# Down projections whose partial sums collect in PSUM, copied out by ScalarE, with weights fetched six steps ahead

## The chip, the cores and the metric

The kernel runs on one core of one Trainium2 chip. The metric is device time in microseconds (us). The kernel before takes 1835.76 us, the median of three runs (1833.45 to 1837.6).

The core has a matrix engine (PE; weight loads are listed as PEld), a vector engine (DVE), a scalar engine (ACT), GpSimd (POOL) and SyncE (SP), which here issues all DMA. Matrix products land in PSUM, which has 8 banks of 128x512 f32. The program names them by what they mostly hold: three `mm`, one `o`, two `y`, two `tp`.

## The reference

One layer of a decoder trunk on a 1024x1024 activation: a gated feed-forward block (FFN), a token mixer with two kinds of attention, a second FFN, each followed by a residual sum and a layer norm (LN). The part that is changed is the last product of each FFN and the sum and LN behind it:

```
def swiglu(h, w_gate, w_up, w_down):
    return (jax.nn.silu(h @ w_gate) * (h @ w_up)) @ w_down
...
        h = modulate(x, sh1, sc1)
        y = swiglu(h, ffn1_w_gate[l], ffn1_w_up[l], ffn1_w_down[l])
        x = layer_norm(ALPHA * x + (1 + g1) * (MACARON * y), ln1_g[l], ln1_b[l])
        h = modulate(x, sh2, sc2)
        y = token_mix(h, w_in[l], b_forget[l], swa_sinks[l], grp_gain[l], w_out[l])
        x = layer_norm(ALPHA * x + (1 + g2) * y, ln2_g[l], ln2_b[l])
        h = modulate(x, sh3, sc3)
        y = swiglu(h, ffn2_w_gate[l], ffn2_w_up[l], ffn2_w_down[l])
        x = layer_norm(ALPHA * x + (1 + g3) * (MACARON * y), ln3_g[l], ln3_b[l])
```

`w_down` has 2816 rows and 1024 columns.

## The kernel before

All large products run as three matmuls of rounded pieces (`mm3`, L105): each operand is split by `split` (L101) into a rounded high part (ACT cast, L102) and a remainder (DVE subtraction, L103), and high x high, high x low and low x high are added in PSUM.

`down` is called once for each FFN (at about 448 us and 1603 us of the trace). It computes A @ B with A = 1024x2816 (stored transposed in device memory, `aT`) and B = `w_down`, as a 2x2 block product in seven half-size products in place of eight. The blocks of A are A11 to A22, of B B11 to B22; S1 to S4 and T1 to T4 are sums of them. This document numbers the products P1 = A11·B11, P2 = A12·B21, P3 = S4·B22, P4 = A22·T4, P5 = S1·T1, P6 = S2·T2, P7 = S3·T3. The results are C11 = P1+P2 (left columns, first 512 tokens), C12 = P1+P6+P5+P3 (right columns, first 512 tokens), C21 = P1+P6+P7 with P4 added or subtracted by the sign of T4 (left columns, last 512 tokens) and C22 = P1+P6+P7+P5 (right columns, last 512 tokens).

Each product has 11 steps (`NG`, one for each 128 rows of the inner dimension), and a step is 4 output banks x 3 matmuls of 128x512. In the last product the last `tail` steps (2 in the first call, 7 in the second) are run bank by bank, so that bank 0 is complete first. A step's operands are made by `operands`: a DMA of an `aT` tile into ring `u`, a DMA or a sum for the weight tile, and two splits into rings `z` (4 buffers) and `w` (6). `get` records the operands one step ahead (`LOOK`), three from the sixth product on. T2, T1 and T4 are made in place over the weight tiles by `weight`.

In the kernel before the order is P1, P2, P3, P6, P5, P7, P4, and the bank sets alternate between products (`PBANKS`). Every product is evicted by itself at its end, bank by bank: P1 and P3 with an ACT copy (L477), the others with one or two DVE sums of PSUM and a 128x2048 SBUF tile (`x1`, `x2`, `x3`, `u4`). Finished results are put on a list `todo`, from which one entry is popped after each step: `add_to` (L420) multiplies by the gate (L423) and adds to the residual (L424); then come the LN of the first 512 tokens (`steps1` in the first call, `final_a` in the second). After the loop the caller does the LN of the last 512 tokens: in the first call `ln_steps` between the blocks of the V projection (L741 to L778), in the second `final_b` (L1302), with which the program ends. `ln_stats` takes two `bn_stats` (left and right half), `bn_aggr`, an epsilon, and a power on POOL.

The order of instructions on each engine is set before the run by the layer that builds the program, from the order in which they are recorded, the buffers' releases and its own estimates; every engine, SP too, then runs its list strictly in that order.

Of the kernel before, what the change touches and what calls it, by code (L numbers as in the profile page):

```python
# [14 lines left out]
P = 128  # L15
# [31 lines left out]
def layer_kernel(ctx, tc, xT, x, c, adaT, adab, wg1, wu1, wd1, wqk, wv1, wv2, bf, sinks,  # L47
# [57 lines left out]
    def mm3(o, lh, ll, rh, rl, start, stop):  # L105
        T.matmul(o, lh, rh, start=start, stop=False)  # L106
        T.matmul(o, lh, rl, start=False, stop=False)  # L107
        T.matmul(o, ll, rh, start=False, stop=stop)  # L108
# [46 lines left out]
    def ln_stats(src):  # L155

        s6 = small([P, 2, 6], "bn", 4)
        V.bn_stats(s6[:, 0], src[:, :HT])
        V.bn_stats(s6[:, 1], src[:, HT:])
        mv = small([P, 2], "mv", 4)  # L160
        V.bn_aggr(mv, s6)
        ve = small([P, 1], "ve", 4)
# [5 lines left out]
    def ln_norm(src):  # L168
        mv, rs = ln_stats(src)
        V.tensor_scalar(src, src, mv[:, 0:1], rs, op0=ALU.subtract, op1=ALU.mult)  # L170
# [194 lines left out]
    def down(ai, wd, gate, alpha, load, steps_a, tail=TAIL):  # L365
# [4 lines left out]
        sums = {}  # L370
# [15 lines left out]

        def weight(kind, g):
            if kind in ("B11", "B21", "B22"):
                return home(kind, g)
            if kind == "T2":  # L390
                b12 = home("B12", g)
                b11, b21, b22 = (raw[k, 0, g] for k in ("B11", "B21", "B22"))
# [10 lines left out]
            return raw[{"T1": "B11", "T3": "B12", "T4": "B21"}[kind], 0, g]  # L403
# [13 lines left out]
        def stash():  # L417
            return st("h", [P, 4, HT])

        def add_to(xt, k, n, s, eng=V):  # L420

            y = xt[k][:, cols[n]]
            eng.tensor_tensor(s, s, gate[:, cols[n]], ALU.mult)  # L423
            V.scalar_tensor_tensor(y, y, alpha, s, op0=ALU.mult, op1=ALU.add)  # L424
# [16 lines left out]
        xs = []  # L441
        for i in range(7):
            banks = [psum(q) for q in PBANKS[2 if i == 6 and not ai else i % 2].split()]

            def mul(a, w, g, k):
                mm3(banks[k], a[:, 0, k * P:(k + 1) * P], a[:, 1, k * P:(k + 1) * P], w[:, 0], w[:, 1],
                    g == 0, g == NG - 1)

            tl = tail if i == 6 else 1
            for g in range(NG - tl):  # L450
                a, w = get(i, g)
                for k in range(4):
                    mul(a, w, g, k)
                if i in (0, 4) and 2 <= g < 6:
                    if g == 2:
                        xs.append([])
                    xs[-1].append(load(i // 4, g - 2))
                if todo:
                    for f in todo.pop(0):
                        f()  # L460
            aw = [get(i, g) for g in range(NG - tl, NG)]
            if i in (0, 1, 2, 4):
                new = stash()
                if i == 0:
                    x1 = new
                elif i == 1:
                    x2 = new
                elif i == 2:
                    x3 = new
                else:  # L470
                    u4 = new
            for k in range(4):
                for j in range(tl):
                    mul(*aw[j], NG - tl + j, k)
                b = banks[k]
                if i in (0, 2):
                    A.copy(new[:, k], b)  # L477
                elif i in (1, 4):
                    V.tensor_tensor(new[:, k], x1[:, k], b, ALU.add)
                    if i == 4:  # L480
                        V.tensor_tensor(x3[:, k], x3[:, k], b, ALU.add)
                elif i == 3:
                    V.tensor_tensor(x1[:, k], x1[:, k], b, ALU.add)
                elif i == 5:
                    V.tensor_tensor(u4[:, k], u4[:, k], b, ALU.add)
                    V.tensor_tensor(x1[:, k], x1[:, k], b, ALU.add)
                else:
                    s = xs[1][k][:, cols[0]]
                    if not ai:
                        V.tensor_tensor(b, b, gate[:, cols[0]], ALU.mult)  # L490
                    V.tensor_tensor(s, s, b, ALU.subtract)
            if i == 1:
                todo = [[lambda k=k: add_to(xs[0], k, 0, x2[:, k])] for k in range(4)]
            elif i == 3:
                todo = [[lambda k=k: V.tensor_tensor(x3[:, k], x3[:, k], x1[:, k], ALU.add)] for k in range(4)]
            elif i == 4:
                todo = [[lambda k=k: add_to(xs[0], k, 1, x3[:, k])] for k in range(4)] + steps_a(xs[0])
            elif i == 5:
                z = [[lambda k=k, n=n: add_to(xs[1], k, n, (x1, u4)[n][:, k], V)] for n in range(2) for k in range(4)]
                for j in range(8):  # L500
                    if j < len(todo):
                        todo[j] = z[j] + todo[j]
                    else:
                        todo.append(z[j])
        while todo:
            for f in todo.pop(0):
                f()
# [172 lines left out]
    def ln_steps(zt, hf, m, dst, split_to, park=None):  # L680

        def norm(k):
            ln_norm(zt[k])
# [37 lines left out]
    def steps1(z):  # L721
# [5 lines left out]
              steps1)  # L727
# [548 lines left out]
    def final_a(zt):  # L1276
# [3 lines left out]
        def stats(k):  # L1280
# [3 lines left out]
            s1, s2, nm, ve = (q[:, j:j + 1] for q in [small([P, 2, 6], "bn", 4)[:, 0]] for j in range(4))  # L1284
# [18 lines left out]
    def final_b(zt):  # L1303
# [20 lines left out]
        for k in range(4):  # L1324
            sc[k] = ln_stats(zt[k])
# [3 lines left out]
    final_b(down(1, wd2, gate_load(2), 1.0, load_x2, final_a, 7))  # L1329
# [59 lines left out]
```

## Time and profile before

| | |
|---|---|
| median of 3 runs | 1835.76 us |
| the profiled execution's own time | 1834.09 us |
| its span, first to last instruction | 1832.1 us |
| granted PE clock, mean over the span | 0.985 of full |
| busy: PE / DVE / ACT | 1755.3 / 1546.1 / 764.7 us |

Busy time is the time in which at least one instruction of the engine is under way. Matmuls overlap: in a dense stretch they start 0.227 us apart and each is shown as 0.39 us long, so a busy PE has no visible gap, and gaps show as a duration in brackets with what ended them. DVE operations on 128x512 start 0.60 us apart and are shown as 0.69 us long.

### The profile page before, as it was taken

The page shows a single profiled execution, that of the slowest core. Times are in us where ns is not written, and L with a number is a line of the kernel's source. Part 1 is how long each engine was busy: PE and PEld are TensorE (multiplying, and loading weights), DVE is VectorE, ACT ScalarE, POOL GpSimd, SP SyncE. Part 2 cuts the span into 40 slices and gives each one's busy share as a digit, 9 for nine tenths or more (in the row PEclk, how much of TensorE's full clock was granted, in tenths as well). Part 3 has the DMA queues.
Part 4 walks back from the last instruction along what each step waited for, and adds up shares of the span by engine and source line. Part 5 has one row for each costly group of instructions (what it writes and reads, how often), then busy time and mean ns, then how long its engine had stood idle before and what let it go on. Part 6 is the DMA issues. An engine that isn't in the chain of part 4 may idle for free.

```text
span 1832.1 us, 23557 instructions
## 1 busy us (share of the span) xinstructions
PE 1755.3 (96%) x8114; PEld 1444.7 (79%) x8114; DVE 1546.1 (84%) x2805; ACT 764.7 (42%) x1465; POOL 23.0 (1%) x32
## 2 busy tenths in 40 slices
PE   7999999999999989999889899999999999999995
PEld 5788888888888879877667777778888888888884
DVE  7999999999597995378678797899788887878999
ACT  5432333233544442277356461543233333344480
POOL 0000000000000000000000000000000000000000
PEclk9999999999999999999989999999999999999998
DMA  9355555558754245855958863333223232675442
GB/s 360 127 197 178 193 193 193 170 173 290 233 167 143 86 134 180 242 148 154 229 143 198 215 205 107 138 109 128 97 99 131 88 108 92 223 231 166 133 144 80
DMA packets 163175, 303.44 MB, mean 166 GB/s; under 512 B 15384, under 2 KB 47728, under 8 KB 163056
## 3 DMA queue, kind: packets, MB, share of 16 engines
q1 hardware_dynamic: 163056, 301.94, 52.1%
q8 instruction: 64, 1.05, 0.2%
q14 instruction: 55, 0.45, 0.1%
HBM read 224.17 MB, written 77.71 MB: 165 GB/s over the span
## 4 chain that ended last, share of the span: by engine, by line
PE 73%; DVE 15%; DMA 6%; ACT 3%; issue 2%; SPq 0%; POOL 0%; DVEq 0%; ACTq 0%; POOLq 0%
PE y L106 10%; PE y L107 10%; PE y L108 10%; PE mm L106 9%; PE mm L108 9%; PE mm L107 9%; PE o L106 3%; PE o L108 3%; PE o L107 3%; DVE w L103 2%; DVE h L103 2%; DMA q<-cum_d 2%; PE tp L107 1%; PE tp L108 1%; PE tp L1114 1%
## 5 line engine op out<-in xcount | busy, mean ns | idle before, releaser
L102 ACT CAST w<-u 128x512 fp32r<-128x512 f32 x303 | 186.6, 622 | 393.1 <-PE y L108 160.2
L106 PE MATMUL y<-h,w 128*128 128x512 f32 x728 | 287.7, 395 | 5.0 <-ACT h L102 2.1
L107 PE MATMUL y<-h,w 128*128 128x512 f32 x728 | 285.6, 392 | 0.0
L108 PE MATMUL y<-h,w 128*128 128x512 f32 x728 | 285.2, 392 | 0.0
L103 DVE TENSOR_TENSOR w<-u,w 128x512 fp32r<-128x512 f32 x303 | 206.5, 686 | 23.4 <-ACT w L102 22.1
L106 PE MATMUL mm<-h,w 128*128 128x512 f32 x528 | 207.7, 394 | 18.7 <-ACT h L102 15.6
L107 PE MATMUL mm<-h,w 128*128 128x512 f32 x528 | 206.7, 392 | 0.3 <-DVE h L103 0.2
L108 PE MATMUL mm<-h,w 128*128 128x512 f32 x528 | 206.7, 392 | 0.0
L106 PEld LDWEIGHTS y<-h,w 128*128 128x128 f32 x728 | 137.5, 189 | 33.5 <-ACT h L102 2.5
L108 PEld LDWEIGHTS y<-h,w 128*128 128x128 f32 x728 | 137.0, 188 | 26.6
L107 PEld LDWEIGHTS y<-h,w 128*128 128x128 f32 x728 | 137.0, 188 | 26.3
L102 ACT CAST w<-t 128x512 fp32r<-128x512 f32 x106 | 65.5, 621 | 185.1 <-PE mm L108 70.3
L106 PEld LDWEIGHTS mm<-h,w 128*128 128x128 f32 x528 | 100.2, 190 | 40.9 <-ACT h L102 16.0
L107 PEld LDWEIGHTS mm<-h,w 128*128 128x128 f32 x528 | 100.0, 189 | 22.2 <-DVE h L103 1.5
L108 PEld LDWEIGHTS mm<-h,w 128*128 128x128 f32 x528 | 99.9, 189 | 21.3 <-DVE w L103 1.0
L102 ACT CAST z<-u 128x512 fp32r<-128x512 f32 x88 | 54.8, 623 | 105.2 <-PE y L108 46.8
L103 DVE TENSOR_TENSOR z<-u,z 128x512 fp32r<-128x512 f32 x88 | 60.5, 689 | 35.7 <-ACT z L102 35.6
L103 DVE TENSOR_TENSOR t<-tp,t 128x512 fp32r<-128x512 f32 (+1 forms) x126 | 72.8, 586 | 18.4 <-ACT t L102 17.7
L102 ACT CAST t<-tp 128x512 fp32r<-128x512 f32 (+1 forms) x126 | 61.8, 502 | 48.3 <-PE tp L1114 47.4
L102 ACT CAST w<-h 128x512 fp32r<-128x512 f32 x111 | 68.2, 617 | 29.4 <-PE o L108 10.5
L103 DVE TENSOR_TENSOR w<-h,w 128x512 fp32r<-128x512 f32 x111 | 75.6, 686 | 1.8 <-ACT w L102 1.8
L103 DVE TENSOR_TENSOR w<-t,w 128x512 fp32r<-128x512 f32 x106 | 72.8, 689 | 1.4 <-ACT w L102 0.8
(356 smaller groups left out, 3948.1 us busy)
## 6 DMA issues: line engine op xcount, KB each, us to landing
u<-aT SPq DMA_DIRECT2D x154, 256.0 KB, 2.7
q<-in_adaT SPq DMA_DIRECT2D x56, 512.0 KB, 3.4
u<-in_wg SPq DMA_DIRECT2D x92, 256.0 KB, 3.0
u<-in_wu SPq DMA_DIRECT2D x90, 256.0 KB, 2.8
aT<-z SPq DMA_DIRECT2D x44, 512.0 KB, 3.2
h<-in_wd SPq DMA_DIRECT2D x88, 256.0 KB, 4.5
qkd<-w SPq DMA_DIRECT2D x26, 512.0 KB, 4.1
aT<-b SPq DMA_DIRECT2D x22, 512.0 KB, 4.2
```

The lines of the kernel that those rows point to most:

```text
L102: A.copy(hi, src)
L103: V.tensor_tensor(lo, src, hi.bitcast(F32), ALU.subtract)
L106: T.matmul(o, lh, rh, start=start, stop=False)
L107: T.matmul(o, lh, rl, start=False, stop=False)
L108: T.matmul(o, ll, rh, start=False, stop=stop)
L1114: T.transpose(pt[:, tok(i - q0)], sps[i][:, tok(j)], ident)
```

## The change

The products run in the order P1, P2, P6, P5, P3, P7, P4. Bank set 0 (`tp tp y y`) takes P1; then P6, P5 and P3 are added into the same four banks without a restart, so that they hold P1, P1+P6, P1+P6+P5 and C12 in turn. Two of these sums on the way are copied out by ACT: `u` (P1, later overwritten by P1+P6) and `u4` (P1+P6+P5). Bank set 1 (`mm mm mm o`) takes P2, and afterwards P7 with P4 added on top; P7 alone is copied out by ACT in between (`p7`). T4 has the other sign, so P4 is added, and both calls multiply the finished P7+P4 by the gate in PSUM (in the second call this takes the place of a multiplication of each T4 tile). C22 is `u4 + p7`, summed on DVE in the function `second`.

The DMAs of B22 and B12 are recorded six steps from the start on, one with each step's operands, in place of with the step that needs them. The `bn_stats` of the right half of the last 512 tokens is taken as soon as C22 is added (`ln_early`), and `ln_stats` then takes only the left half. Some ring sizes of small tiles are 2 in place of 4 (`bn`, `ve`). In the V projection the first two blocks use `y` banks. In the last product of each call three entries of the list are popped before each bank's gate.

```
-    def mm3(o, lh, ll, rh, rl, start, stop):
-        T.matmul(o, lh, rh, start=start, stop=False)
...
+    def mm3(o, lh, ll, rh, rl, start, stop, more=False):
+
+        T.matmul(o, lh, rh, start=start, stop=False, skip_group_check=more)
...
-    def ln_stats(src):
-
-        s6 = small([P, 2, 6], "bn", 4)
+    begun_stats = {}
+
+    def ln_early(k, src):
+
+        begun_stats[k] = small([P, 2, 6], "bn2", 4)
+        V.bn_stats(begun_stats[k][:, 1], src[:, HT:])
+
+    def ln_stats(src, k=None):
+
+        s6 = begun_stats.pop(k, None)
+        if s6 is None:
+            s6 = small([P, 2, 6], "bn", 2)
+            V.bn_stats(s6[:, 1], src[:, HT:])
         V.bn_stats(s6[:, 0], src[:, :HT])
-        V.bn_stats(s6[:, 1], src[:, HT:])
...
-    DOWN = (("A11", "B11"), ("A12", "B21"), ("S4", "B22"), ("S2", "T2"), ("S1", "T1"), ("S3", "T3"), ("A22", "T4"))
-    PBANKS = ("tp tp y y", "mm mm mm o", "y y mm mm")
+    DOWN = (("A11", "B11"), ("A12", "B21"), ("S2", "T2"), ("S1", "T1"), ("S4", "B22"), ("S3", "T3"), ("A22", "T4"))
+    PBANKS = {0: "tp tp y y", 1: "mm mm mm o", 5: "mm mm mm o"}
+    AHEAD = 6
...
+        coming = [(kind, g) for kind in ("B22", "B12") for g in range(NG)]
...
                 t = st("t", [P, HT])
                 V.tensor_tensor(t, b22, b11, ALU.subtract)
-                V.tensor_tensor(b21, t, b21, ALU.subtract)
+                V.tensor_tensor(b21, b21, t, ALU.subtract)
                 return t
             if kind == "T1":
-                b12, b21 = raw["B12", 0, g], raw["B21", 0, g]
-                V.tensor_tensor(b12, raw["B22", 0, g], b12, ALU.subtract)
-                if ai:
-                    V.tensor_tensor(b21, b21, gate[:, cols[0]], ALU.mult)
...
+                V.tensor_tensor(b12, b22, b12, ALU.subtract)
...
                 j, h = plan[len(made)]
+                if len(made) >= AHEAD and coming:
+                    home(*coming.pop(0))
                 made.append(operands(*DOWN[j], h, ring(j, h)))
...
         for i in range(7):
-            banks = [psum(q) for q in PBANKS[2 if i == 6 and not ai else i % 2].split()]
+            if i in PBANKS:
+                sets[i in (1, 5)] = [psum(q) for q in PBANKS[i].split()]
+            banks = sets[i in (1, 5, 6)]
+            more = i not in PBANKS
...
                 if i in (0, 2):
-                    A.copy(new[:, k], b)
-                elif i in (1, 4):
-                    V.tensor_tensor(new[:, k], x1[:, k], b, ALU.add)
-                    if i == 4:
-                        V.tensor_tensor(x3[:, k], x3[:, k], b, ALU.add)
+                    A.copy(u[:, k], b)
+                elif i == 1:
+                    V.tensor_tensor(c[:, k], u[:, k], b, ALU.add)
                 elif i == 3:
-                    V.tensor_tensor(x1[:, k], x1[:, k], b, ALU.add)
+                    A.copy(u4[:, k], b)
                 elif i == 5:
-                    V.tensor_tensor(u4[:, k], u4[:, k], b, ALU.add)
-                    V.tensor_tensor(x1[:, k], x1[:, k], b, ALU.add)
-                else:
+                    A.copy(p7[:, k], b)
+                elif i == 6:
+                    for _ in range(3):
+                        pop()
                     s = xs[1][k][:, cols[0]]
-                    if not ai:
-                        V.tensor_tensor(b, b, gate[:, cols[0]], ALU.mult)
-                    V.tensor_tensor(s, s, b, ALU.subtract)
+                    V.tensor_tensor(b, b, gate[:, cols[0]], ALU.mult)
+                    V.tensor_tensor(s, s, b, ALU.add)
             if i == 1:
-                todo = [[lambda k=k: add_to(xs[0], k, 0, x2[:, k])] for k in range(4)]
-            elif i == 3:
-                todo = [[lambda k=k: V.tensor_tensor(x3[:, k], x3[:, k], x1[:, k], ALU.add)] for k in range(4)]
+                todo = [[lambda k=k: add_to(xs[0], k, 0, c[:, k])] for k in range(4)]
             elif i == 4:
-                todo = [[lambda k=k: add_to(xs[0], k, 1, x3[:, k])] for k in range(4)] + steps_a(xs[0])
+                todo = [[lambda k=k, b=banks[k]: add_to(xs[0], k, 1, c[:, k], b)] for k in range(4)] + steps_a(xs[0])
             elif i == 5:
-                z = [[lambda k=k, n=n: add_to(xs[1], k, n, (x1, u4)[n][:, k], V)] for n in range(2) for k in range(4)]
+                def second(k):
+                    V.tensor_tensor(u4[:, k], u4[:, k], p7[:, k], ALU.add)
+                    add_to(xs[1], k, 1, u4[:, k])
+                    if early:
+                        early(k, xs[1][k])
+                z = [[lambda k=k: second(k)] for k in range(4)]
+                z += [[lambda k=k: add_to(xs[1], k, 0, u[:, k])] for k in range(4)]
...
-                p = psum("mm")
+                p = psum("y" if hf + pz == 0 and k < 2 else "mm")
...
-            sc[k] = ln_stats(zt[k])
+            sc[k] = ln_stats(zt[k], k)
```

Three places in the engines' lists. The first is DVE at the end of the program, before: the rows begin with the last bank of the last product (`y_15805`) being added to the residual of the fourth token tile (`z_15374`); `z_15294`, `z_15321`, `z_15348` are the other three.

```order
L491 TENSOR_TENSOR z_15374<-z_15374,y_15805 128x512
L159 BN_STATS s_bn_16029<-z_15294 128x6
L158 BN_STATS s_bn_16038<-z_15321 128x6
L161 BN_AGGR s_mv_16032<-s_bn_16029 128x2
L159 BN_STATS s_bn_16038<-z_15321 128x6
L163 TENSOR_SCALAR s_ve_16034<-s_mv_16032 128x1
L158 BN_STATS s_bn_16047<-z_15348 128x6
L161 BN_AGGR s_mv_16041<-s_bn_16038 128x2
L159 BN_STATS s_bn_16047<-z_15348 128x6
L163 TENSOR_SCALAR s_ve_16043<-s_mv_16041 128x1
L158 BN_STATS s_bn_16056<-z_15374 128x6
L161 BN_AGGR s_mv_16050<-s_bn_16047 128x2
```

Now, the same place: `o_15433` is the last bank of the last product, `z_15327` the fourth token tile, `z_15279` and `z_15303` the second and third.

```order
L505 TENSOR_TENSOR o_15433<-o_15433,b_14139 128x512
L1333 TENSOR_TENSOR z_15279<-z_15279,h_15555 128x512
L506 TENSOR_TENSOR z_15327<-z_15327,o_15433 128x512
L1334 TENSOR_TENSOR z_15279<-z_15279,h_15555 128x512
L169 BN_STATS s_bn_2977_15844<-z_15327 128x6
L1331 SCALAR_TENSOR_TENSOR s_nb_16018<-s_mv_15989,s_rs_15993 128x1
L1337 SCALAR_TENSOR_TENSOR z_15303<-z_15303,s_rs_15993,h_15555 128x512
L171 BN_AGGR s_mv_15996<-s_bn_2977_15844 128x2
L173 TENSOR_SCALAR s_ve_15998<-s_mv_15996 128x1
L1336 SCALAR_TENSOR_TENSOR z_15327<-z_15327,s_mv_15996,h_15555 128x512
L1333 TENSOR_TENSOR z_15303<-z_15303,h_15555 128x512
L1337 SCALAR_TENSOR_TENSOR z_15327<-z_15327,s_rs_16000,h_15555 128x512
```

Before, the statistics of all four tiles and their whole normalisation stand behind the last bank; now those of the first two tiles and half of the third's stand ahead of it, and three rows are left behind the rows shown (L1334, L1336, L1337).

The second place is SP's list of DMAs behind the first `down`: `in_wv` are the V projection's weights (320 columns the first kind, 328 the second), `in_lnrow` a row vector of the first LN whose buffer is the gate's. Before:

```order
L739 DMA u_5637<-in_wv 128x320
L739 DMA u_5641<-in_wv 128x320
L150 DMA b_5721<-in_lnrow 128x1024
L739 DMA u_5646<-in_wv 128x328
L739 DMA u_5650<-in_wv 128x328
L739 DMA u_5654<-in_wv 128x328
```

Now:

```order
L757 DMA u_5621<-in_wv 128x320
L757 DMA u_5626<-in_wv 128x328
L757 DMA u_5630<-in_wv 128x328
L757 DMA u_5634<-in_wv 128x328
L757 DMA u_5639<-in_wv 128x328
L757 DMA u_5643<-in_wv 128x328
L757 DMA u_5647<-in_wv 128x328
L757 DMA u_5652<-in_wv 128x328
L151 DMA b_5693<-in_lnrow 128x1024
L757 DMA u_5656<-in_wv 128x328
```

The row vector has moved from ahead of all eight loads of the second kind to behind seven of them.

The third place is ACT at the end of P5 in the first `down`, now: the four copies of P1+P6+P5 out of banks into which P3 is then added.

```order
L102 CAST w_4787<-u_4789 128x512
L498 COPY h_4750<-tp_3726 128x512
L102 CAST h_4975<-h_4112 128x512
L498 COPY h_4750<-tp_3727 128x512
L498 COPY h_4750<-y_3728 128x512
L498 COPY h_4750<-y_3729 128x512
L102 CAST w_4788<-h_3852 128x512
```

Before, that place has no ACT copy: the banks of P5 were added on DVE, and the next product had other banks.

## Rows read from the trace of the kernel before

**Rows 1.** The page's busy time by engine: us, share of the span, instructions.
```profile
PE 1755.3 (96%) x8114; PEld 1444.7 (79%) x8114; DVE 1546.1 (84%) x2805; ACT 764.7 (42%) x1465; POOL 23.0 (1%) x32
```

**Rows 2.** Busy time by stretch: from:to, length, each engine's busy us (instructions), PE clock, DMA.
```profile
448.00:661.00 213.00, 213.00 (x956) 175.99 (x955) 175.98 (x296) 99.77 (x177) 2.96 (x4) 1.00 0.51 157
661.00:671.60 10.60, 10.60 (x73) 10.46 (x71) 9.70 (x23) 4.72 (x10) 0.55 (x1) 1.00 0.60 176
671.60:684.00 12.40, 6.58 (x29) 5.74 (x28) 10.39 (x23) 2.69 (x5) 1.65 (x3) 0.72 0.66 209
...
1812.70:1828.60 15.90, 0.00 (x0) 0.00 (x0) 15.89 (x36) 2.44 (x3) 2.94 (x4) 0.63 0.24 99
1828.60:1832.10 3.50, 0.00 (x0) 0.00 (x0) 0.00 (x0) 0.00 (x0) 0.00 (x0) 0.50 0.39 150
```

**Rows 3.** PE's waits, 661 to 700 us: us in total, times, longest.
```profile
PE tp L185 <- DVE z L170: 5.8, 3, 3.2
```

**Rows 4.** PE's waits, 1601 us to the end.
```profile
PE tp L107 <- DVE h L103: 1.5, 1, 1.5
```

**Rows 5.** DVE instructions in order of time: start, us, what [idle before].
```profile
668.32 1.88 DVE L741 TENSOR_TENSOR h<-u,h 128x328 fp32r<-128x328 f32 x4 [0.90 <-ACT h L740]
...
671.59 0.81 DVE L170 TENSOR_SCALAR z<-z,s_mv,s_rs 128x1024 f32<-128x1024 f32 x1
672.32 0.49 DVE L741 TENSOR_TENSOR h<-u,h 128x328 fp32r<-128x328 f32 x1
...
1812.78 0.68 DVE L491 TENSOR_TENSOR z<-z,y 128x512 f32<-128x512 f32 x1
...
1823.33 0.75 DVE L1319 SCALAR_TENSOR_TENSOR z<-z,s_rs,h 128x512 f32<-128x512 f32 x1
1823.99 0.69 DVE L1315 TENSOR_TENSOR z<-z,h 128x512 f32<-128x512 f32 x1
1824.59 0.75 DVE L1319 SCALAR_TENSOR_TENSOR z<-z,s_rs,h 128x512 f32<-128x512 f32 x1
```

**Rows 6.** PE in order of time, behind the V projection's third block.
```profile
672.55 0.30 PE L185 MATMUL tp<-ident,z 128*128 128x128 f32 x1 [0.78 <-DVE z L170]
...
679.75 0.47 PE L108 MATMUL mm<-h,h 128*128 128x320 f32 x1
680.01 0.47 PE L106 MATMUL mm<-h,h 128*128 128x320 f32 x1
...
683.76 0.31 PE L107 MATMUL mm<-h,h 128*128 128x320 f32 x1
683.90 0.30 PE L108 MATMUL mm<-h,h 128*128 128x320 f32 x1
```

**Rows 7.** ACT in order of time, the row vector of the first LN.
```profile
666.62 1.06 ACT L152 ACTIVATE b<-b 128x1024 f32<-128x1024 f32 x1 [6.17 <-DMA b<-in_lnrow]
```

**Rows 8.** SP in order of time, its load's issue.
```profile
662.55 0.33 SPq L150 DMA_DIRECT2D b<-in_lnrow  x1
```

**Rows 9.** PE in order of time, end of P3 and start of P6.
```profile
535.29 0.39 PE L108 MATMUL tp<-w,z 128*128 128x512 f32 x1
...
537.56 0.39 PE L106 MATMUL mm<-w,z 128*128 128x512 f32 x1
```

**Rows 10.** ACT in order of time, there.
```profile
535.72 0.59 ACT L477 COPY h<-tp 128x512 f32<-128x512 f32 x1
536.20 0.62 ACT L102 CAST h<-h 128x512 fp32r<-128x512 f32 x1
536.72 0.59 ACT L477 COPY h<-tp 128x512 f32<-128x512 f32 x1
```

**Rows 11.** ACT in order of time, casts of the first `down`'s last product.
```profile
619.36 0.62 ACT L102 CAST w<-u 128x512 fp32r<-128x512 f32 x1 [4.30 <-PE o L108]
```

**Rows 12.** PE in order of time, behind the second LN.
```profile
1189.73 0.51 PE L106 MATMUL y<-h,w 128*128 128x512 f32 x1 [2.10 <-ACT h L102]
```

**Rows 13.** DVE's busy time in the second `down`, in P2 (columns as Rows 2).
```profile
1640.00:1650.00 10.00, 10.00 (x45) 8.26 (x44) 4.94 (x8) 3.69 (x8) 0.00 (x0) 1.00 0.30 83
```

More of the change, by code (lines that the diff above doesn't have):

```diff
@@ L103, in split @@
         V.tensor_tensor(lo, src, hi.bitcast(F32), ALU.subtract)
-    def mm3(o, lh, ll, rh, rl, start, stop):
-        T.matmul(o, lh, rh, start=start, stop=False)
-        T.matmul(o, lh, rl, start=False, stop=False)
-        T.matmul(o, ll, rh, start=False, stop=stop)
+    def mm3(o, lh, ll, rh, rl, start, stop, more=False):
+        T.matmul(o, lh, rh, start=start, stop=False, skip_group_check=more)
+        T.matmul(o, lh, rl, start=False, stop=False, skip_group_check=more)
+        T.matmul(o, ll, rh, start=False, stop=stop, skip_group_check=more)
     def halves(t):
@@ L358, in gate_up, with down @@
         a_store(ai, NG - 1, a)
-    DOWN = (("A11", "B11"), ("A12", "B21"), ("S4", "B22"), ("S2", "T2"), ("S1", "T1"), ("S3", "T3"), ("A22", "T4"))
-    PBANKS = ("tp tp y y", "mm mm mm o", "y y mm mm")
-    def down(ai, wd, gate, alpha, load, steps_a, tail=TAIL):
+    DOWN = (("A11", "B11"), ("A12", "B21"), ("S2", "T2"), ("S1", "T1"), ("S4", "B22"), ("S3", "T3"), ("A22", "T4"))
+    PBANKS = {0: "tp tp y y", 1: "mm mm mm o", 5: "mm mm mm o"}
+    AHEAD = 6
+    def down(ai, wd, gate, alpha, load, steps_a, tail=TAIL, early=None):
         cols = [slice(0, HT), slice(HT, D)]
@@ L369, in down @@
         mixed = {}
-        sums = {}
         def home(kind, g):
@@ L385, in home @@
             return t
+        coming = [(kind, g) for kind in ("B22", "B12") for g in range(NG)]
         def weight(kind, g):
-            if kind in ("B11", "B21", "B22"):
+            if kind in ("B11", "B21"):
                 return home(kind, g)
+            b11, b21, b22, b12 = (raw.get((k, 0, g)) for k in ("B11", "B21", "B22", "B12"))
             if kind == "T2":
-                b12 = home("B12", g)
-                b11, b21, b22 = (raw[k, 0, g] for k in ("B11", "B21", "B22"))
                 V.tensor_tensor(b11, b12, b11, ALU.subtract)
@@ L441, in down, with pop @@
         xs = []
+        sets = {}
+        def pop():
+            if todo:
+                for f in todo.pop(0):
+                    f()
         for i in range(7):
-            banks = [psum(q) for q in PBANKS[2 if i == 6 and not ai else i % 2].split()]
+            if i in PBANKS:
+                sets[i in (1, 5)] = [psum(q) for q in PBANKS[i].split()]
+            banks = sets[i in (1, 5, 6)]
+            more = i not in PBANKS
             def mul(a, w, g, k):
                 mm3(banks[k], a[:, 0, k * P:(k + 1) * P], a[:, 1, k * P:(k + 1) * P], w[:, 0], w[:, 1],
-                    g == 0, g == NG - 1)
+                    g == 0 and not more, g == NG - 1, more)
             tl = tail if i == 6 else 1
@@ L457, in down @@
                     xs[-1].append(load(i // 4, g - 2))
-                if todo:
-                    for f in todo.pop(0):
-                        f()
+                pop()
             aw = [get(i, g) for g in range(NG - tl, NG)]
[L462 to L469, printed above, removed]
-                else:
-                    u4 = new
+            if i == 0:
+                u = stash()
+            elif i == 1:
+                c = stash()
+            elif i == 3:
+                u4 = stash()
+            elif i == 5:
+                p7 = stash()
             for k in range(4):
@@ L505, in down @@
         while todo:
-            for f in todo.pop(0):
-                f()
+            pop()
         return xs[1]
@@ L726, in layer_kernel @@
     xb = down(0, wd1, gate_load(0), ALPHA, load_x1,
-              steps1)
+              steps1, early=ln_early)
     vd = dram([10, S, P], "vd")
@@ L1283, in stats @@
             nb, rs = small([P, 1], "nb", 4), small([P, 1], "rs", 4)
-            s1, s2, nm, ve = (q[:, j:j + 1] for q in [small([P, 2, 6], "bn", 4)[:, 0]] for j in range(4))
+            s1, s2, nm, ve = (q[:, j:j + 1] for q in [small([P, 2, 6], "bn", 2)[:, 0]] for j in range(4))
             A.activation(zt[k], zt[k], AF.Identity, accum_out=s1)
```

19 lines of the change are left out of this document (10 added, 9 removed).

## The prediction

> **What bounds the kernel now.** I read the page's totals first: PE is busy 96% of the span and DVE 84% [rows 1]. An average over stages says little, so next the stretches. Through the first `down` PE has no gap at all in 213 us, while DVE has 37 us to spare [rows 2]. There a DVE instruction less is worth nothing. Then the waits of PE: the only large one around the first `down` comes behind it, 5.8 us in three pieces for the normalised tiles of the LN [rows 3], and in the second `down` there is one of 1.5 us for a split [rows 4]. Last the end: PE's last matmul is over at 1812.7, DVE then works 15.9 us without a gap, and 3.5 us later the last store has landed [rows 2, 5]. So the change can earn at three places only: the tail behind the last matmul (19.4 us), the LN behind the first `down`, and the 1.5 us.
>
> **DVE work taken away.** Per call, 28 DVE sums (evictions of P2, P6, P5, P7 and four on the list) become 8 (four for P2, four `u4+p7`), against 8 more ACT copies of 0.59 us [rows 10]. At 0.60 us from start to start (1823.99 to 1824.59 [rows 5]) this frees 20 x 0.60 = 12 us of DVE per call; in the second, 11 gate products on T4 tiles become 4 in the banks, another 4.2 us. I cost the seven products themselves at nothing: the same 924 matmuls, hidden behind PE as now. What counts is whether DVE arrives earlier at the three places.
>
> **The tail.** PE starts a matmul each 0.227 us (ten steps from 535.29 to 537.56 [rows 9]). P7's last matmul stands 132 matmuls before the end of the new list, 29.9 us. From the first `u4+p7` to the last split that PE needs there are 32 DVE operations, 19.3 us. P7's copies of the first two banks can be there about 30.5 us before the end, so that split is done 11.2 us before the end; PE needs it 11.3 before it (50 matmuls). That is just in time: I take 0.2 us of waiting, between 0 and 2, in place of the 1.5 us now. Then bank 0 is complete 10.9 us before the end, bank 1 9.5, bank 2 4.8, and DVE's list goes through them with little slack: by the end it has finished the first tile and stands before the last bank. Behind the last bank remain 12 operations of 128x512, 7 at 0.60 and 5 of the two-scalar kind at 0.66 (1823.33 to 1823.99 [rows 5]), together 7.5 us, some 0.3 us of small ones and 0.4 us from the last matmul's start to the first of them: 8.2 us, against 15.9. The store's 3.5 us stay. So the end comes at 1812.7 - 1.5 + 0.2 + 8.2 + 3.5 = 1823.1, 9.0 us earlier. If DVE is late by 3 us at the last bank the gain is 6; if it waits nowhere, 9.5.
>
> **The LN behind the first `down`.** Now: behind the last bank DVE has the residual sums, weight splits and the statistics to do, and in between waits 0.90 us for ACT [rows 5], which had been held 6.17 us by one load [rows 7]. That load was issued at 662.55, when the gate's buffer came free [rows 8], and eight weight loads stood behind it on SP. PE has finished three blocks at 671.6 and waits 0.78 and then most of 5 us more for four tiles [rows 3, 6]. After it the matmuls of 320 columns run 0.267 us apart in place of 0.147 (72 steps in 10.6 us [rows 2]) until 683.6: 17 x 0.12 = 2.0 us, at a mean clock of 0.72 for the stretch [rows 2, 6].
> After the change half of each tile's statistics is done before the last bank, seven of the eight loads no longer stand behind the gate, and two blocks more have banks. DVE's load from P7's end to the last bank is nearly unchanged: 8 evictions go (-4.8), `u4+p7` and the early statistics come (+4.8), and six splits and one product of the row vector move ahead (+3.6); counted along the list, it ends the last bank's gate at 660.8 to 662, where P4 itself ends at 661.2. From there: two residual sums 1.2, six splits 2.5, two statistics 1.2; then a split of the last load, which ACT can cast at about 6.5 us (the row vector's 4.1 us from issue to landing [rows 7, 8], its 1.06 us product and the cast); aggregation, the next statistics and POOL's power, which I estimate at 1.9, and the normalisation, 0.73 (671.59 to 672.32 [rows 5]). The first tile is ready about 10.0 us after the product, the others at 10.7, 12.1 and 13.3. PE's list wants the first at 61 matmuls x 0.147 = 9.0 us, so it waits 1.05, then 0.1 and 0.5: 1.6 us in place of 5.8, and I take the clock as kept. Gain 5.8 - 1.6 + 2.0 = 6.2; bounds: nothing (the wait stays whole) and 7.8.
>
> **The second LN.** The smaller rings for `bn` and `ve` also reorder the LN behind the mixer: in PE's list the transposes of its last four tiles start 8 matmuls later, 1.8 us. There PE waits on the splits that follow them, 2.1 us at one place [rows 12]. A delay passes on at most whole; cost 0 to 1.8, I take 1.0.
>
> **Waits that are added.** P5 and P3 continue in banks that ACT must first have copied, likewise P4 behind P7: three boundaries per call. A bank's next matmul starts 2.27 us after its last one did, and the copy starts 0.43 us after that and takes 0.59, so 1.25 us of slack per bank [rows 9, 10]. ACT is in order; in the new list one cast stands between the copies, as it did here [rows 10], so I take 0. The early DMAs move no byte more and come earlier; they can at worst delay B11's tiles, where the lists are equal up to step 7: 0, at most 1.
> The Trainium skill, "Perfetto Trace Analysis", section "Matmuls", asks for the opposite: independent groups of matmuls should rotate through different PSUM banks so that evacuation overlaps the next group. By that rule each of the six boundaries costs the whole 1.02 us of lag and copy for the first bank, if nothing of it were hidden, some 6 us by the rows above; the trace says the other three banks' nine matmuls hide it. No run here shows such a boundary yet.
>
> **Sum.** -9.0 - 6.2 + 1.0 = -14.2 us. The profiled execution's own time is 1834.09, 1.99 above its span, so 1819.9 on its scale; it lies 1.7 under the median, and the median's scale gives 1835.76 - 14.2 = 1821.6. I predict 1821.5.
>
> **Rivals.**
> (a) The LN's wait stays, since the last row vector still gates the eighth split and ACT; only the tail gains: 1835.8 - 9.0 + 1.0 = 1828. For it: the load still waits for the gate's buffer. Against: only one split of 16 is behind it. Chance 0.14.
> (b) Slower: the reused banks stall PE. If a copy stands behind a cast that itself waits for a release, it is late: ACT waits of 4.30 us before a cast occur in this very stage [rows 11]. Then each of six boundaries costs 4.30 - 1.25 = 3.05 us, 18.3 in all: 1840. It decides from (14.2 / 6) + 1.25 = 3.6 us of lateness on. Against: the casts next to the copies are of operands long released. Chance 0.08 for it, half of that on the slower side.
> (c) T2's sums, now directly behind P2, starve PE: P6's steps need 5 operations, 3.0 us, against 2.72 of PE, and 8 operations of the first result come on top: 33.1 + 4.8 - 29.9 = 8.0 us short per call, 16 in all: 1837.5. Against: DVE is half idle during P2 [rows 13], and in the second call's list 20 of the 33 sums stand ahead of the first of these splits. Chance 0.06.
> (d) All goes well, no wait at the LN, none at the end: 1835.8 - 9.5 - 7.8 = 1818.5, or a little less. Chance 0.12.
>
> **Chances and range.** The forecast has 0.60. Within 0.2% (3.7 us), about what a measurement of this kernel can tell from no change, lie most of (c) and a part of (a) and (b): 0.08. Slower: half of (b), a part of (c) and what I don't see: 0.07. Faster: 0.85. The range for 8 in 10 goes from 1814.5, under (d) by what the estimates may miss, to 1831, which takes in (a) and a milder (b); the likeliest case alone spans 1817 to 1826.
>
> **What would show it.** Right: DVE's work behind the last matmul is 8 to 9 us; PE's wait on the normalisation behind the first `down` is under 2.5 us and no slow matmuls follow; no PE wait on an ACT copy. Wrong: PE waits on L494, L498 or L500 (b); PE waits on splits during P6 (c); the wait on the LN is still near 6 us (a); or DVE reaches the last bank late, with 12 us or more behind it.

## The result and the profile after

The changed kernel takes 1818.42 us (median of 4 runs, 1816.05 to 1819.7) against 1834.62 us for the kernel before beside it: a ratio of 0.9908, 95% interval 0.9891 to 0.9925, or 16.2 us less. Run again later it gave 0.9911 (0.9895 to 0.9926). The prediction was 1821.5 us. The profiled execution has an own time of 1819.7 us, its span is 14.3 us shorter than that of before.

Where the 14.3 us are is read from three of PE's rows that both kernels have: the first matmul of 328 columns (behind the LN of the first `down`), the first matmul of the second `down`, and the last matmul. Start, us, what. Before:

```profile
685.28 0.40 PE L106 MATMUL mm<-h,h 128*128 128x328 f32 x1
...
1599.94 0.39 PE L106 MATMUL tp<-w,z 128*128 128x512 f32 x1
...
1812.29 0.39 PE L108 MATMUL y<-h 128*128 128x512 f32 x1
```

After:

```profile
677.72 0.40 PE L107 MATMUL mm<-h,h 128*128 128x328 f32 x1
...
1592.98 0.39 PE L107 MATMUL tp<-w,z 128*128 128x512 f32 x1
...
1805.36 0.39 PE L109 MATMUL o<-h 128*128 128x512 f32 x1
```

The same kernel in the later run:

```profile
678.21 0.40 PE L107 MATMUL mm<-h,h 128*128 128x328 f32 x1
...
1588.10 0.39 PE L107 MATMUL tp<-w,z 128*128 128x512 f32 x1
...
1800.09 0.39 PE L109 MATMUL o<-h 128*128 128x512 f32 x1
```

The first is 7.56 us earlier after the change, the second 6.96, the third 6.93, and from the third to the end it is 12.44 us in place of 19.81. So the gain is 7.5 us behind the first `down` and 7.4 behind the last matmul; the second `down` takes the same time. Between the first and second row lie the mixer, the second LN and the first products of the second FFN, called the mixer here. It takes 914.7 us before, 915.3 after and 909.9 in the later run of the same kernel: a difference of some 5 us there is no reading of an edit, and comparisons below are made by ratios and by stretches outside it.

The page's busy time after, to [rows 1]:

```profile
PE 1751.8 (96%) x8114; PEld 1441.9 (79%) x8114; DVE 1518.1 (84%) x2758; ACT 771.8 (42%) x1481; POOL 23.0 (1%) x32
```

Busy time by stretch after (columns as in [rows 2]; the last two are the tail's two pieces):

```profile
448.00:661.00 213.00, 213.00 (x956) 176.09 (x955) 170.42 (x287) 106.21 (x191) 2.58 (x4) 1.00 0.52 161
661.00:671.60 10.60, 10.21 (x70) 9.78 (x69) 10.17 (x26) 2.74 (x5) 1.50 (x3) 1.00 0.70 231
671.60:684.00 12.40, 12.23 (x85) 11.68 (x85) 11.81 (x20) 5.53 (x9) 1.03 (x2) 1.00 0.58 199
1805.75:1814.27 8.52, 0.00 (x1) 0.00 (x0) 8.45 (x16) 0.81 (x1) 1.79 (x2) 0.77 0.33 135
1814.27:1817.80 3.53, 0.00 (x0) 0.00 (x0) 0.00 (x1) 0.00 (x0) 0.00 (x0) 0.50 0.40 160
```

Through the first `down` PE is without a gap as before. From 671.6 to 684 it is busy 12.23 us in place of 6.58, with 85 matmuls in place of 29, at the full clock. Behind the last matmul DVE works 8.5 us in place of 15.9.

PE's waits after, first from 655 to 700 us and then from 1601 to the end, to [rows 3, 4]:

```profile
PE tp L195 <- DVE z L180: 0.4, 1, 0.4
...
PE mm L108 <- DVE h L103: 1.7, 1, 1.7
```

The LN's wait went from 5.8 to 0.4 us. The wait for a split in the second `down` did not go: 1.7 us, where it was 1.5. A shorter one early in the second `down`, which [rows 4] leaves out, is 0.6 us before (at 1606.55) and 0.8 after (at 1599.80). No wait on a copy (L494, L498, L500) is listed in either call.

SP, ACT and DVE behind the first `down` after, in order of time, to [rows 5, 7, 8]:

```profile
653.82 7.15 SPq L757 DMA_DIRECT2D u<-in_wv  x6
662.41 0.33 SPq L151 DMA_DIRECT2D b<-in_lnrow  x1
...
666.15 1.06 ACT L153 ACTIVATE b<-b 128x1024 f32<-128x1024 f32 x1 [0.91 <-DMA b<-in_lnrow]
...
663.49 2.55 DVE L759 TENSOR_TENSOR h<-u,h 128x328 fp32r<-128x328 f32 x6
665.95 1.29 DVE L169 BATCH_NORM_STATS2 s_bn<-z 128x6 f32<-128x512 f32 x2
...
669.63 1.70 DVE L180 TENSOR_SCALAR z<-z,s_mv,s_rs 128x1024 f32<-128x1024 f32 x2
```

The row vector's load still waits for the gate, but ACT is held 0.91 us by it, not 6.17. The splits of 320 columns are gone from behind the last bank (they were done inside the `down`), and two tiles are normalised by 671.3, when before had not begun the first [rows 5].

The boundary P6 to P5 after, where the next product goes on in the same banks, ACT and then PE, to [rows 9, 10]:

```profile
535.58 0.62 ACT L102 CAST w<-h 128x512 fp32r<-128x512 f32 x1
536.10 1.07 ACT L494 COPY h<-tp 128x512 f32<-128x512 f32 x2
...
535.26 0.39 PE L109 MATMUL tp<-w,z 128*128 128x512 f32 x1
...
537.53 0.39 PE L107 MATMUL tp<-w,z 128*128 128x512 f32 x1
```

The last matmul in the first bank starts at 535.26, the copy at 536.10 behind a cast; with 0.59 us for one copy it ends at 536.7, and PE is back in this bank at 537.53. No PE wait stands at this boundary or at the five others of its kind.

### The profile page after: what moved, and what is told of

It reads as the page before. It is cut to its first block, busy times and chain, and to the rows that moved or that the text cites. A ratio compares the mean times of both kernels' runs of the same rounds, so it can differ in the third digit from the quotient of the medians.

```text
span 1817.8 us, 23527 instructions
## 1 busy us (share of the span) xinstructions
PE 1751.8 (96%) x8114; PEld 1441.9 (79%) x8114; DVE 1518.1 (84%) x2758; ACT 771.8 (42%) x1481; POOL 23.0 (1%) x32
## 4 chain that ended last, share of the span: by engine, by line
PE 78%; DVE 11%; DMA 5%; ACT 3%; issue 2%; POOL 0%; SPq 0%; DVEq 0%; ACTq 0%; POOLq 0%
PE y L107 11%; PE y L109 11%; PE y L108 11%; PE mm L109 9%; PE mm L108 9%; PE mm L107 9%; PE o L107 3%; PE o L108 3%; PE o L109 3%; PE tp L107 2%; PE tp L109 2%; PE tp L108 2%; DVE h L103 2%; DMA q<-cum_d 2%; PE tp L1132 1%
## 5 line engine op out<-in xcount | busy, mean ns | idle before, releaser
L103 DVE TENSOR_TENSOR w<-u,w 128x512 fp32r<-128x512 f32 x303 | 206.8, 688 | 24.1 <-ACT w L102 22.4
L103 DVE TENSOR_TENSOR t<-tp,t 128x512 fp32r<-128x512 f32 (+1 forms) x126 | 72.7, 587 | 19.1 <-ACT t L102 18.3
L102 ACT CAST w<-h 128x512 fp32r<-128x512 f32 x111 | 68.4, 618 | 29.9 <-DMA h<-in_wd 15.3
```

The source lines that it names most:

```text
L102: A.copy(hi, src)
L103: V.tensor_tensor(lo, src, hi.bitcast(F32), ALU.subtract)
```

## The experiments

Each ratio is to runs of the kernel before on the same chip. The first `down` runs from its first matmul to the V projection's first, the stretch LN from there to the V projection's first matmul of 328 columns, the tail from the last matmul's start to the end; all three are from the one profile of each run, in us.

| run | ratio (95%) | first `down`, longer by | LN | tail |
|---|---|---|---|---|
| before | 1 | 0 | 24.1 | 19.8 |
| the changed kernel | 0.9908 (0.9891 to 0.9925) | -0.1 | 16.6 | 12.4 |
| the same again | 0.9911 (0.9895 to 0.9926) | -0.1 | 17.5 | 12.4 |
| collecting undone | 0.9969 (0.9956 to 0.9982) | -0.1 | 21.6 | 19.2 |
| collecting alone | 0.9924 (0.9909 to 0.9939) | 0.9 | 16.9 | 13.2 |
| no early statistics | 0.9906 (0.9884 to 0.9927) | -0.1 | 16.1 | 11.3 |
| no pops | 0.9916 (0.9890 to 0.9942) | -0.1 | 17.0 | 14.5 |
| fetched with the step | 0.9937 (0.9916 to 0.9957) | 1.2 | 16.9 | 12.4 |
| V in `mm` banks | 0.9912 (0.9895 to 0.9928) | -0.1 | 16.4 | 12.4 |
| DVE copies | 0.9955 (0.9940 to 0.9970) | 2.8 | 16.8 | 14.3 |
| copies three times | 0.9959 (0.9943 to 0.9975) | 2.7 | 17.8 | 12.8 |
| row vector, kernel before | 1.0038 (1.0026 to 1.0049) | 0.0 | 23.4 | 19.8 |
| POOL in the tail | 0.9922 (0.9903 to 0.9941) | -0.1 | 16.9 | 11.0 |
| early statistics in one call | 0.9910 (0.9895 to 0.9926) | -0.1 | 16.4 | 11.3 |

**Collecting undone.** Each product has banks of its own again and goes out through DVE:

```
-    PBANKS = {0: "tp tp y y", 1: "mm mm mm o", 5: "mm mm mm o"}
+    PBANKS = ("mm mm mm o", "tp tp y y")
...
+                elif i == 2:
+                    V.tensor_tensor(u[:, k], u[:, k], b, ALU.add)
...
-                    A.copy(u4[:, k], b)
+                    V.tensor_tensor(u4[:, k], u[:, k], b, ALU.add)
...
+                elif i == 4:
+                    V.tensor_tensor(c[:, k], u4[:, k], b, ALU.add)
                 elif i == 5:
-                    A.copy(p7[:, k], b)
+                    V.tensor_tensor(u4[:, k], u4[:, k], b, ALU.add)
+                    V.tensor_tensor(u[:, k], u[:, k], b, ALU.add)
```

> Order of the products, early statistics, prefetch and pops as in the changed kernel, but every product has its own banks and is summed out on DVE: 16 DVE sums more and 12 ACT copies less per call. Theory (the DVE time freed inside the call counts only because DVE reaches the last bank with less left to do): the LN's wait behind the first down is back at 4 us or more, and all of the last LN but the right halves' statistics stands behind the last matmul, 13 to 14 us of DVE instead of 8.5; in all 1828 to 1832. Rival (the early statistics and the pops did it, collecting in PSUM gives nothing): 1818 to 1821.

Two thirds of the gain went: 0.9969, or 1828.9 us on the scale of 1834.62. PE's waits from 655 to 700 us, and DVE's stretch behind the last matmul:

```profile
PE y L108 <- DVE h L759: 2.4, 1, 2.4
PE tp L195 <- DVE z L180: 1.7, 1, 1.7
PE mm L107 <- DVE z L507: 0.2, 1, 0.2
...
1808.80:1824.11 15.31, 0.00 (x1) 0.00 (x0) 15.27 (x34) 2.41 (x3) 2.48 (x4) 0.66 0.25 103
```

4.3 us of waits are back, the largest for a split of the V projection's weights, which DVE had not come to; those for the normalised tiles are 1.7 us of them. The tail is 15.3 us of DVE again, longer than the 13 to 14 expected. The theory holds in the main. The third of the gain that stays belongs to all the rest together: the order of the products, the 7 gate products fewer in the second call, early statistics, pops and early fetch.

**Collecting alone** is the counterpart: no early statistics, no pops, weights fetched with the step, V in `mm` banks, small rings of 4. What the collecting is built on stays in: the new order of the products, T4's sign and the gate on the finished P7+P4. No run has these without the collecting and without the other parts.

> The new order of products, the collecting in PSUM and the ACT copies alone: no early statistics, no pops before a gate, weights fetched with their step, V projection in the mm banks, small rings of 4 as before. Theory (collecting alone brings nearly all: DVE then has the V projection's splits behind it when the last bank comes, and reaches the tail's last bank with one tile and a half left): 0 to 3 us above the changed kernel, the LN's wait behind the first down under 2 us. Rival (the parts need each other, since separate undoing of each showed little because the others covered it): 5 us or more above the changed kernel.

It keeps 0.9924; its distance to the changed kernel beside it is 0.13%, 2.4 us, inside both intervals, as the theory has it. PE's only wait from 655 to 700 us:

```profile
PE tp L195 <- DVE z L180: 0.7, 1, 0.7
```

The tail is 0.7 us longer than in the changed kernel. The row vector's load stands behind seven weight loads here too, so that move needs none of the parts left out.

**Early statistics** undone in both calls (`early=ln_early` and the last argument of the second call left out), and in the second call only:

> The changed kernel with both halves' statistics taken together, as before. Theory: in the first call four statistics of 0.60 us stand behind the last bank again, the fourth LN tile comes 2.4 us later and PE's wait goes from 0.4 to about 2; in the second call DVE works without a gap either way, so moving four statistics is worth little there, and the 1.7 us PE waits for a split 16 us before the end goes away because they stood ahead of it. In all 1819 to 1822. Rival (the early statistics are what shortens LN and tail): 4.8 us and more, 1823 to 1827.

> The changed kernel with the early statistics only in the first call. Theory (in the second call the four statistics stand ahead of splits that PE waits for, and DVE has a gap behind these that they can fill): PE's wait of 1.7 us before the end falls under 1, the DVE list behind the last matmul is 7 to 8 us, and it is 1 to 3 us faster than the changed kernel. Rival (as good as without any early statistics): no difference from the changed kernel, within 1 us.

Neither differs from the changed kernel (0.9906 and 0.9910). The LN's wait is 0.9 us without them, not 2: half of the first theory fell. DVE's list shows why: C22 is finished ahead of C21 in the new order, and without being recorded early two of the four statistics of the right halves move ahead of the last bank in the first call (all four with collecting alone) and all four in the second. The other half, PE's wait before the end, is open. It was 0.8 us in both runs, against 1.7 and 1.2 in the changed kernel; but it was also 0.6 with V in `mm` banks and 0.7 with the weights fetched with the step, which both keep the early statistics. What differs is the tail: 11.3 us with the early statistics out of the second call, 12.4 in those four runs with them. That is too little for the ratio.

**Pops** undone (`for _ in range(3): pop()` left out):

> The changed kernel without the three list entries taken before each bank's gate. Theory: the first call's list is empty by then, so nothing there; in the second, three more DVE operations of 0.60 us are left behind the last matmul: 1.8 us, about 1820. Rival (only the order on DVE differs, its work is the same): 1818.4, no difference.

The tail is 2.1 us longer, as the theory says, but PE's wait for the split fell from 1.7 to 0.3 us. The work is the same and stands in another order; the ratio cannot tell.

**Weights fetched with the step** (`coming = []`, B22 and B12 loaded by T2):

> The changed kernel with B22 and B12 fetched with the step that needs them (both with T2's steps) instead of six steps on. Theory (SP's list is set from buffer releases and the loads of 2.7 to 5.4 us fit in a step or two; PE has no wait for them in the kernel before): 0 to 2 us, 1818 to 1821. Rival (two loads per step in P6 come late, T2's sums wait for them and PE starves): 0.5 us and more in each of 11 steps and two calls, 1829 or more.

DVE's waits in the first `down`, the one that is new:

```profile
DVE h L406 <- DMA h<-in_wd: 6.4, 5, 2.3
```

T2's first sums wait for loads in five places, 6.4 us; PE loses 1.2 us, in the first call only. The ratio is further off, but its interval reaches that of the changed kernel. So the early fetch is worth about 1 us by the profile, and whether it is worth more is open.

**V projection in `mm` banks** (`psum("mm")` for all blocks):

> The changed kernel with all blocks of the V projection in the mm banks. Theory (P4's banks are read out by DVE from 657 to 663 us, the first mm bank before the block that wants it; the fourth block needs the first block's sum on DVE, which ended at 671.9): PE waits 0 to 1 us, no difference that can be measured. Rival (the y banks let PE go on while DVE was behind, and are part of the gain at the LN): 3 to 6 us slower.

0.9912, and no PE wait at all between 655 and 700 us. The `y` banks bring nothing that can be measured.

**Copies by DVE** (`V.tensor_copy` in place of `A.copy` for P1+P6, P1+P6+P5 and P7):

> The changed kernel with the three intermediate copies of a call (P1+P6, P1+P6+P5, P7) made by DVE instead of ACT: 12 DVE operations of 0.60 us more per call, and the next product's first matmul in a bank now waits for DVE's list instead of ACT's. Theory (a bank has 1.25 us to spare, DVE's list is in order and has splits and sums queued): PE waits at the boundaries on DVE's copies, and the LN and the tail get part of the 7.2 us per call back; 1825 to 1833. Rival (DVE has 30 us of idle time in a call and the copies fit into it): 1817 to 1820.

0.9955, 1826.4 on the scale of 1834.62, where the theory put it. PE waits on copies now, 1.6 us on L494 and 0.5 on L498 in the first call and 0.5 on L500 in the second; the first `down` is 2.8 us longer, the tail 1.9; the stretch LN did not get longer (16.8). Who copies matters. At P6's end DVE's first copy starts at 538.41, behind sums and splits, where ACT's started at 536.10; in the changed kernel's first `down` ACT is busy 106 of 213 us and DVE 170.

**Copies three times over** (the three intermediate `A.copy` in loops of three; P1's stays single):

> The changed kernel with each of the three intermediate copies of a call made three times over by ACT (the same copy repeated, so the banks come free later). Theory (four banks in turn leave 2.27 us from a bank's last matmul to its next; copies start every 0.50 us on ACT): the fourth bank is copied 0.43 + 12 x 0.50 + 0.5 for a cast = 6.9 us after the first bank's last matmul, PE wants it at 4.3, so about 2.6 us at each of six boundaries, 15 us in all, 1830 to 1836, with waits on the copies in the profile. Rival 1 (each boundary pays the whole lag already): 8 copies x 0.50 more at each of six, 24 us, 1842. Rival 2 (a bank's reuse isn't what PE waits for): 1818 to 1821.

0.9959, or 1827.1, between the theory and rival 2. PE behind the boundary P6 to P5:

```profile
537.54 0.39 PE L109 MATMUL y<-w,z 128*128 128x512 f32 x1
538.92 0.50 PE L107 MATMUL tp<-w,z 128*128 128x512 f32 x1 [0.99 <-ACT h L495]
...
541.79 0.39 PE L107 MATMUL tp<-w,z 128*128 128x512 f32 x1
542.02 0.39 PE L107 MATMUL y<-w,z 128*128 128x512 f32 x1
```

It waits 1.0 us once, then runs 13 matmuls in the `tp` banks before it touches a `y` bank: the program's layer put matmuls of the next step ahead while the `y` banks are copied. Five of the six boundaries show such a wait, of 0.6 to 1.0 us, 4.1 in all. The sum of 2.6 us per boundary took PE's order as fixed, and at this boundary it is not. Against the changed kernel's first profile the two `down` are 2.7 and 2.9 us longer, the stretch LN 1.1 and the tail 0.4.

**Row vector, in the kernel before** (`rows2(0, ALPHA)` in place of `rows2(0, ALPHA, "b")`):

> The kernel before with one edit: the first LN's row vectors go to a buffer that does not wait for the gate, and their loads stand behind all of the V projection's weights. Theory (the held load costs DVE only its own two short gaps of 0.90 and 0.67 us; the rest of the LN's wait is work left to DVE): PE's wait falls from 5.8 to 4 or 5, gain 1 to 3 us, 1832 to 1834. Rival (the order of loads on SP is what made the LN late): the wait falls under 2 us and the slow matmuls behind it go, gain 5 to 7, 1828 to 1830.

Both missed: it became slower. PE's waits from 665 us on, and what stands behind the last:

```profile
672.96 0.41 PE L185 MATMUL tp<-ident,z 128*128 128x128 f32 x2 [1.31 <-DVE z L170]
674.93 0.44 PE L185 MATMUL tp<-ident,z 128*128 128x128 f32 x2 [1.56 <-DVE z L170]
677.24 0.63 PE L106 MATMUL mm<-h,h 128*128 128x320 f32 x1 [1.87 <-DVE w L762]
...
706.97 0.31 PE L107 MATMUL mm<-h,h 128*128 128x320 f32 x1
711.62 0.63 PE L108 MATMUL mm<-h,h 128*128 128x320 f32 x1 [4.34 <-DVE h L708]
712.05 0.47 PE L106 MATMUL mm<-h,h 128*128 128x320 f32 x1
712.32 0.47 PE L107 MATMUL mm<-h,h 128*128 128x320 f32 x1
```

The LN's own wait fell to 2.9 us, but a block's eviction (1.87 us) took the place of part of it, and with the late row vectors the residual's scaling (L673 and L674, on DVE until 710.8) stands ahead of splits that PE wants at 707: 4.34 us and slow matmuls behind. So the order of loads alone was not the cause: in the stretch LN it is worth 0.7 us. That the edit moved other work besides is why its total says nothing on the theory.

**POOL in the tail**, with the early statistics in the first call only:

```
-                    V.tensor_tensor(y, y, r3[0][:, cs], ALU.mult)
-                    V.tensor_tensor(y, y, r3[1][:, cs], ALU.add)
+                    e = G if k else V
+                    e.tensor_tensor(y, y, r3[0][:, cs], ALU.mult)
+                    e.tensor_tensor(y, y, r3[1][:, cs], ALU.add)
```

> The changed kernel with two edits at its end: the early statistics only in the first call, and for the second and third of the last four tiles the two sums of the right half on POOL instead of DVE. Theory (behind the last matmul only DVE's list counts): 4 operations of 0.60 us leave it, 2.4 us, beside up to 2 us for the statistics that stood ahead of the last splits; 1814 to 1816. Rival (POOL's operations are long and the last tile's power, which POOL does behind them, comes late): no gain or 1 to 3 us more than without, 1816 to 1820.

0.9922: no gain, and the tail is 11.0 us against 11.3 without POOL. Four operations left DVE, but the last bank's gate came late. In the run with the early statistics in one call it starts at 1800.84, with the end of the last matmul (1800.81); here it starts 1.9 us behind that end (1806.73 and 1804.79; the rows are in the last section).

No version beat the changed kernel by more than the ratios can tell.

## Why the prediction was right, and where its steps were off

**The places** were right: 7.5 us of the gain are behind the first `down` and 7.4 behind the last matmul, and 28 us less of DVE time over the span (1546.1 to 1518.1) bought nothing inside the products. The cause was right too: collecting in PSUM takes work from DVE, so DVE comes to the last bank with less left. Collecting alone, with the order, sign and gate that it is built on, brings 0.76% of the changed kernel's 0.89%, and undoing it with these kept takes away 0.58%.

**The sum** is close by luck. The prediction took 9.0 + 6.2 - 1.0 = 14.2 us off, and the two profiles differ by 14.3: 7.4 at the end and 7.5 at the LN, less 0.6 in the mixer. The end came 1.6 us short, the LN 1.3 over, and the mixer, where the 1.0 was expected, differs by 5 us between two runs of one kernel. The medians are 16.2 us apart.

**The tail** was predicted at 8.2 us of DVE; it is 8.5, with the 12 operations of 128x512 that the prediction counted. Ahead of the last bank's gate stand the statistics of three tiles and half of the fourth's, more than the section on the change says. DVE after, its first and last operations behind the last matmul, and the last store:

```profile
1806.18 0.69 DVE L505 TENSOR_TENSOR o<-o,b 128x512 f32<-128x512 f32 x1
...
1813.52 0.75 DVE L1337 SCALAR_TENSOR_TENSOR z<-z,s_rs,h 128x512 f32<-128x512 f32 x1
1814.30 0.33 SPq L1339 DMA_DIRECT2D out<-z  x1
```

**PE's wait before the end** is the mis-sized term: 0.2 us predicted (0 to 2), 1.7 measured, and 1.2 in the later run. Of the 9.0 us predicted at the end 1.3 were to come from this wait and 7.7 from the tail; nothing came from the first and 7.4 from the second. The sum looked only at the last split and set it against PE. That one was in time; DVE finished all splits at 1793.9, 11.8 us before the last matmul's end. Late was one in the middle. DVE, then PE:

```profile
1788.43 0.70 DVE L433 SCALAR_TENSOR_TENSOR z<-z,h 128x512 f32<-128x512 f32 x1
1789.03 0.70 DVE L103 TENSOR_TENSOR h<-h,h 128x512 fp32r<-128x512 f32 x1
...
1789.79 0.50 PE L108 MATMUL mm<-h 128*128 128x512 f32 x1 [1.75 <-DVE h L103]
```

A residual sum of C22 (1788.43) stands ahead of the split, which ends at 1789.7. How late that is varies: with V in `mm` banks, whose second call has the same code, the wait was 0.6 us.

**The LN** was mis-sized the other way: a wait of 1.6 us predicted, 0.4 here and 1.3 in the later run; the first tile was ready 9.4 us after the product, not 10.0. With the clock kept (2.0 us, as predicted) the stretch LN is 7.5 and 6.6 us shorter in the two runs; predicted were 6.2. One reason given for it was too large: the early `bn_stats` counted as half of the statistics moved ahead, and two of these four (all four with collecting alone) move ahead without the edit.

**The second LN** was priced at +1.0 for the smaller rings. PE's waits there are not longer: 2.1 us at the place of [rows 12], unchanged, and on the transposes 1.6 and 1.4 us in the two runs, where it was 1.5. Collecting alone, with rings of 4, has the same 2.1 and 1.6. A cost elsewhere in the mixer is not settled, since two runs of one kernel are 5 us apart there, but none was seen.

**What was priced at nothing.** Bank reuse: right, with no wait at six boundaries, and 0.8 us to spare for the first bank at the boundary shown. The Trainium skill ("Perfetto Trace Analysis", section "Matmuls") would rotate independent groups through different banks; by that rule the prediction put some 6 us on these boundaries, and the changed kernel's two profiles show 0. T2's sums: no PE wait, but DVE has no time to spare from 505 to 531 us, where they are made:

```profile
505.00:531.00 26.00, 26.00 (x117) 21.52 (x116) 26.00 (x44) 10.98 (x20) 0.00 (x0) 1.00 0.34 92
```

The early fetch was priced at 0 and is worth about 1 us: without it those sums wait for loads.

**The rivals.** (a), the LN's wait stays, and (c), T2 starves PE, are not in the profile. (b)'s waits on copies come when DVE copies, at three boundaries and 2.6 us in all, not the 18.3 of (b). (d), all goes well, was nearest in time, 1818.5 against 1818.4, but by another sum: its end was to gain 9.5, and gained 7.4.

## What to carry to other kernels

An engine that is off the path inside a stage still pays at the stage's end: look at how much of its list is left when the last product comes, and count what is taken from its whole list, since a planner that orders by release moves later work forward into the time that comes free. When an edit has several parts, run the main part alone as well as undoing each: here the main part made nearly all of the gain, and the others, undone one at a time, could not be told from nothing by the ratios. Against a consumer's list set every item, not only the last: the middle one was late.

## What the runs showed of the hardware

POOL and DVE slowed each other. POOL, and DVE at the same time, in the kernel with POOL in the tail:

```profile
1802.01 1.29 POOL L1334 TENSOR_TENSOR z<-z,h 128x512 f32<-128x512 f32 x1 [1.47 <-DMA out<-z]
1803.38 1.62 POOL L1335 TENSOR_TENSOR z<-z,h 128x512 f32<-128x512 f32 x1
1804.96 0.99 POOL L175 TENSOR_TENSOR s_rs<-s_ve,nhalf 128x1 f32<-128x1 f32 x1
...
1802.26 1.59 DVE L1338 SCALAR_TENSOR_TENSOR z<-z,s_rs,h 128x512 f32<-128x512 f32 x1
...
1806.73 0.69 DVE L505 TENSOR_TENSOR o<-o,b 128x512 f32<-128x512 f32 x1
```

These two operations on 128x512 (L1334, L1335) took POOL 1.29 and 1.62 us, the next two, at 1807.07 and 1808.42, 1.27 and 1.26; on DVE one takes 0.69. The DVE operation beside the first took 1.59 us where such a one takes 0.75. The Trainium skill ("SBUF — State Buffer", section "SBUF: two separate sides") says that such a pair of operations shares one port as an exclusive lock; the 1.59 us agree with a wait for POOL's 1.29 to end (1803.30), 0.55 us ahead of its own end. The power of 128x1 was slowed without any sum on POOL: in the changed kernel's tail it takes 0.90 us where a two-scalar DVE operation of 128x512 started 0.26 us ahead of it (POOL at 1805.78, DVE at 1805.52), and 0.55 us beside statistics (1794.45 in the kernel with POOL in the tail). So the 0.99 us here are no more than 0.1 us dearer than in the changed kernel.

PE's clock: in the kernel before with the moved row vector, 320-column matmuls ran 0.267 us apart (712.05 to 712.32) behind a gap of 4.34 us, in place of 0.147, and the granted clock of the stretch fell to 0.66, a mean between its two levels (2.4 and 1.2 GHz). Behind gaps of 2.4 and 1.7 us some 10 us apart, with collecting undone, it stayed at 1.00. The two stretches, in this order:

```profile
710.00:720.00 10.00, 8.38 (x40) 8.38 (x41) 4.81 (x8) 1.28 (x3) 0.00 (x0) 0.66 0.38 137
...
661.00:684.00 23.00, 18.47 (x118) 16.56 (x117) 20.43 (x46) 8.92 (x19) 2.21 (x4) 1.00 0.67 208
```

So 4.3 us of waiting in one gap brought slow matmuls, and 4.3 us in three pieces brought none; before, 5.8 us in three pieces within 7 us did [rows 3, 6]. A wait can so cost more than its own length: there the slow matmuls cost 2.0 us on top.
